# Band attention of a hybrid encoder layer: values as weights in two column halves for the prompt, column groups of 32 for the sample

## Chip, core and metric

The kernel runs on one core of one Trainium2 chip. The metric is the device time of one execution in microseconds (us). Three timed runs of the kernel before gave a median of 3266.02 us (3258.2 to 3266.6). One further execution was profiled; all rows below are from it.

## What is computed

One inference step of a one-layer encoder: 2048 prompt tokens (16 tiles of 128) and 8 x 16 sample tokens (one tile). Three residual sub-layers follow each other: a mixer with band attention (8 heads x 64) beside a convolution branch, cross-attention into 256 memory tokens, and an MLP. The change touches the band attention alone. Of the reference:

```python
def band_attn_prompt(q, k, v, table):      # per chunk of 64 queries, a band of 9 chunks of keys
    ...
    s = jnp.einsum('bnqhd,bnkhd->bnhqk', qc, kb).astype(jnp.float32) * (Dh ** -0.5)
    s = s + rel_bias(table, q_off, k_off).astype(jnp.float32)[None, None]
    s = jnp.where(key_valid[None, :, None, None, :], s, NEG_INF)
    p = jax.nn.softmax(s, axis=-1).astype(v.dtype)
    o = jnp.einsum('bnhqk,bnkhd->bnqhd', p, vb)
...
def band_attn_sample(q, k_all, v_all, table):   # 16 queries, 128 cached keys and 16 new ones
    s = jnp.einsum('bqhd,bkhd->bhqk', q, k_all).astype(jnp.float32) * (Dh ** -0.5)
    s = s + rel_bias(table, jnp.arange(T) + past, jnp.arange(L)).astype(jnp.float32)[None]
    p = jax.nn.softmax(s, axis=-1).astype(v_all.dtype)
    o = jnp.einsum('bhqk,bkhd->bqhd', p, v_all)
```

## The kernel before

The mixer takes the first 1010 us or so of the span, the tail of its output projection runs to about 1200 us beside the first cross-attention work, and the MLP fills the second half. Prompt tokens go in four quarters `q` of four tiles; the sample tile rides with quarter 0. For each quarter the input projection (`in_parts`, line L122) writes Q, K and V to scratch in DRAM (`Qd`, `Kd`, `Vd`), VectorE works off the 31 taps of the convolution (L451), and the attention of the quarter before is woven in between. `Plan` gives every small function a due time; sorted by it they are the program order, and a scheduler then sets the order on each engine, which holds at run time.

Most products run as three passes in fp32r (`mm3`: high x high, high x low, low x high). Those of the attention's second half are plain float32 matmuls, and each of them shows as two records of TensorE, with a weight load each.

Prompt attention, `attn(q)`: 32 steps, head `h` by head, tile `i` by tile. A step is `scores` (L564, into the only buffer `sc`; L568 on VectorE adds the bias and takes the minimum, L571 on ScalarE the exponential with its row sum), a step later `xpose` (L585, up to five 128x128 transposes of the probabilities; L587 copies them out), and another step later `values` (L597). There the transposed probabilities are the stationary operand, 128 wide, and 64 columns of V move past them: up to five matmuls a step, 560 in all. After a head's four steps VectorE divides by the row sums (L604). `attn_load` fetches a head's Q, K, V and bias ahead.

Sample attention, `sattn`: per stream `b` the cached keys are transposed (L653) and split, the new keys (L646) and the queries (L647) are loaded, GpSimd spreads the queries over a zeroed block `Q` (L642, L650), `sattn_scores` does 4 x 3 passes over 256 columns, and `sattn_values` (L689) does eight float32 matmuls with 128 wide V as the stationary operand and 32 moving columns.

The cross-attention of the sample tokens, which the change leaves alone, already uses column groups: `s_scores` (L927, tile `ssc`) and `s_values` (L965, tile `so`) give four matmuls with 32 columns of weights each the positions 0, 32, 64 and 96 of the array.

Of the kernel before, what the change touches and what calls it, by code (L numbers as in the profile page):

```python
# [73 lines left out]
class Kern:  # L74
# [93 lines left out]
    def mixer(self):  # L168
# [4 lines left out]
        with ExitStack() as st:  # L173
# [42 lines left out]
            def bias_tables():  # L216
# [14 lines left out]
                for h in range(H):  # L231
                    hk = mp.tile([P, 2, P], F32, tag="av", name="hk")
# [11 lines left out]
                hs = mp.tile([P, 2, P], F32, tag="av", name="hs")  # L244
# [284 lines left out]
            A, KQ, PEND, READY = {}, {}, [], []  # L529

            def attn_load(q, h):
                def fn():
# [8 lines left out]
                    vt = mp.tile([P, 8, HD], F32, tag="av", name="av")  # L541
# [3 lines left out]
                    ss = mp.tile([P, 4], F32, tag="ass", name="ass")  # L545
                    KQ[q, h] = (qt, kt, vt, bt, ss, k0)
                return fn

            def scores(q, h, i):
                def fn():  # L550
# [20 lines left out]
                    nc.scalar.activation(pr[:, :n], tt[:, :n], AF.Exp, bias=mn, scale=-1.0, accum_out=ss[:, i:i + 1])  # L571
# [5 lines left out]
            def xpose():  # L577
                q, h, i, pr, n, jo = PEND.pop(0)
                nj = n // P
                pt = mp.tile([P, 5, P], F32, tag="apt", name="apt")  # L580
# [7 lines left out]
                READY.append((q, h, i, pt, nj, jo))  # L588

            def values():  # L590
                q, h, i, pt, nj, jo = READY.pop(0)
                qt, kt, vt, bt, ss, k0 = KQ[q, h]
                if i == 0:
                    OC[q, h] = ps.tile([P, 4, HD], F32, tag="oc", name="oc")
                oc = OC[q, h]
                for j in range(nj):
                    nc.tensor.matmul(oc[:, i, :], pt[:, j, :], vt[:, jo + j, :], start=j == 0, stop=j == nj - 1)  # L597
                if i == 3:
                    if h % 2 == 0:
                        A[q] = mp.tile([P, 4, P], F32, tag="a", name="a")  # L600
                    r = mp.tile([P, 4], F32, tag="ar", name="ar")
                    nc.vector.reciprocal(r, ss)
                    c = (h % 2) * HD
                    nc.vector.tensor_tensor(A[q][:, :, c:c + HD], oc, r.unsqueeze(2).to_broadcast([P, 4, HD]), op=ALU.mult)  # L604
                    if h % 2:
                        t0 = QT[q][0]
                        nc.sync.dma_start(catd[t0 * P:(t0 + 4) * P, (h - 1) * HD:(h + 1) * HD].rearrange("(i p) c -> p i c", p=P), A[q])

            def attn(q):
                fns = [attn_load(q, 0)]  # L610
                for n in range(4 * H + 2):
                    h, i = n // 4, n % 4
                    if n < 4 * H:
                        fns.append(scores(q, h, i))
                    if 0 < n <= 4 * H:
                        fns.append(xpose)
                    if n > 1:
                        fns.append(values)
                    if i == 2 and h + 1 < H:
                        fns.append(attn_load(q, h + 1))  # L620
                return fns

# [3 lines left out]
            def sattn_prep():  # L626
                SA["vn"] = vn = mc.tile([P, DA], F32, tag="svn", name="svn")
                nc.sync.dma_start(vn, Vd[NTP * P:].rearrange("t h d -> t (h d)"))
                SA["aT"] = mp.tile([P, 4, P], F32, tag="saT", name="saT", bufs=1)

            def sattn_load(b):
                def fn():
                    tok = NTP * P
# [4 lines left out]
                    K = mp.tile([P, 4, 2, 256], F32R, tag="ak", name="sk")  # L638
                    Q = mp.tile([P, 4, 2, P], F32R, tag="sqb", name="sq")
                    qs = mp.tile([P, 4, 2, 16], F32, tag="a", name="qs")  # L640

                    nc.gpsimd.memset(fr(Q), 0.0)  # L642
# [11 lines left out]
                    self.split(K[:, :, 0, 0:P], K[:, :, 1, 0:P], pt.rearrange("p (j t) -> p j t", j=4))  # L654
                    SA[b] = (K, Q, cv)
                return fn

            def sattn_scores(b):
                def fn():
                    K, Q, cv = SA[b]  # L660
# [17 lines left out]
            def sattn_values(b):  # L678
                def fn():
# [4 lines left out]
                    PT = mp.tile([P, 2, P], F32, tag="apt", name="spt")  # L684
                    nc.scalar.activation(PT.rearrange("p s c -> p (s c)"), tp[:, :256], AF.Copy)
                    ov = ps.tile([P, 4, 32], F32, tag="oc", name="ov")
                    for p in range(4):
                        for s, vt in ((0, V), (1, SA["vn"])):
                            nc.tensor.matmul(ov[:, p], vt[:, p * P:(p + 1) * P], PT[:, s, p * 32:(p + 1) * 32], start=s == 0, stop=s == 1)  # L689
                    for j in range(2):  # L690
                        rs = slice(j * HD, (j + 1) * HD)
                        nc.vector.tensor_copy(SA["aT"][rs, :, b * 16:(b + 1) * 16], ov[rs, :, j * 16:(j + 1) * 16])
                    if b == 7:
                        tq = ps.tile([P, 512], F32, tag="tp", name="tpo", bufs=TPB)
                        for p in range(4):
                            nc.tensor.transpose(tq[:, p * P:(p + 1) * P], SA["aT"][:, p, :], self.ident)
                        so = mp.tile([P, DA], F32, tag="t512", name="so")
                        nc.scalar.activation(so, tq, AF.Copy)
                        nc.sync.dma_start(catd[NTP * P:, 0:DA], so)
# [714 lines left out]
```

## Time and profile before

| | |
|---|---|
| median of three runs | 3266.02 us |
| the profiled execution | 3256.27 us, span 3254.5 us |
| TensorE busy (matmul / weight load) | 96% / 82% of the span |
| VectorE, ScalarE, GpSimd busy | 56%, 38%, 19% |
| granted TensorE clock, mean | 0.985 of full speed |
| float32 value matmuls of the prompt (L597) | 1120 records, 319.5 to 1007.3 us |
| value matmuls of the sample (L689) | 128 records, 236.7 to 314.8 us |

Busy shares are averages over stages with different limits; what counts for the change is the stretch from about 210 us to 1010 us. A matmul's duration in a record holds its latency, so a rate is read from the starts of successive groups.

### The profile page before, as it was taken

To read this page: it belongs to the slowest core of one execution; us is meant where nothing else is said; L and a number is where in the kernel's file an instruction comes from. 1 tells how busy PE (TensorE), PEld (TensorE's weight loads), DVE (VectorE), ACT (ScalarE), POOL (GpSimd) and SP (SyncE) were. 2 spreads that over 40 slices of the span, in tenths; PEclk is the share of its full clock that TensorE was granted. 3 is DMA by queue.
4 is the path that set the end of the run, shared out by engine and by line. 5 is a ranking of instruction groups with operands and counts; after the bars stand their busy time and mean duration, and the time that the engine had idled before them with its cause. 6 is when DMAs were issued, how large, how long until landed. Compare 5 with 4: busy or idle time off the path is not lost. (4 is left out here: it accounts for less than half of the span.)

```text
span 3254.5 us, 44695 instructions
## 1 busy us (share of the span) xinstructions
PE 3129.9 (96%) x16664; PEld 2679.6 (82%) x16664; DVE 1827.2 (56%) x2812; ACT 1234.0 (38%) x2499; POOL 614.6 (19%) x704
## 2 busy tenths in 40 slices
PE   8889999999899999999999999999999999999998
PEld 7787788979898768788888999988888888888887
DVE  6798979788634435433335444455445544465444
ACT  3223454534554435422224232333334333343332
POOL 4346253342313320022221000002000200020000
PEclk9999999999899999999999999999999999999999
DMA  5465766747864565322224222234233432243222
GB/s 188 122 175 159 210 171 166 195 122 193 241 176 160 189 202 180 102 65 66 64 86 148 81 75 81 75 107 151 93 104 118 145 104 95 91 142 123 91 94 75
DMA packets 309352, 425.18 MB, mean 131 GB/s; under 512 B 62984, under 2 KB 177680, under 8 KB 309062
## 3 DMA queue, kind: packets, MB, share of 16 engines
q1 hardware_dynamic: 300574, 391.38, 40.5%
q0 software_dynamic: 8560, 30.94, 2.4%
q8 instruction: 131, 2.15, 0.3%
q14 instruction: 87, 0.71, 0.1%
HBM read 356.60 MB, written 69.52 MB: 131 GB/s over the span
## 5 line engine op out<-in xcount | busy, mean ns | idle before, releaser
L122 PE MATMUL pu<-xT,wu 128*128 128x512 f32 (+1 forms) x3840 | 756.3, 358 | 3.2 <-DVE xT L95 2.5
L122 PE MATMUL pd<-wd,h 128*128 128x512 f32 x3264 | 750.6, 390 | 1.4 <-DVE y L1336 1.1
L122 PEld LDWEIGHTS pu<-xT,wu 128*128 128x128 f32 x3840 | 659.9, 188 | 95.8 <-DVE xT L95 2.7
L122 PEld LDWEIGHTS pd<-wd,h 128*128 128x128 f32 x3264 | 611.3, 188 | 129.8 <-DVE y L1336 1.5
L122 PE MATMUL pm<-xT,w 128*128 128x512 f32 (+3 forms) x1992 | 423.2, 363 | 11.8 <-POOL w L95 6.2
L451 DVE SCALAR_TENSOR_TENSOR acc<-u,wdT,acc 128x512 f32<-128x512 f32 x480 | 429.7, 895 | 6.4
L103 POOL TENSOR_SCALAR nm<-nss 128x1 f32<-128x1 f32 x103 | 29.7, 288 | 2025.8 <-ACT nsq L132 1078.6
L122 PEld LDWEIGHTS pm<-xT,w 128*128 128x128 f32 x1992 | 337.6, 194 | 52.0 <-POOL w L95 6.5
L94 ACT ACTIVATE wd<-wst 128x512 fp32r<-128x512 f32 x256 | 159.8, 631 | 430.9 <-PE pd L122 364.5
L95 POOL TENSOR_TENSOR w<-wst,w 128x512 fp32r<-128x512 f32 x154 | 229.1, 1502 | 319.9 <-ACT w L94 296.2
L1336 DVE TENSOR_TENSOR y<-pd,y 128x512 f32<-128x512 f32 x238 | 163.5, 688 | 205.0 <-PE pd L122 204.9
L1318 DVE SCALAR_TENSOR_TENSOR hh<-pu,r 128x512 f32<-128x512 f32 (+1 forms) x160 | 96.8, 609 | 321.1 <-ACT r L1317 320.9
L1317 ACT ACTIVATE r<-pu 128x512 f32<-128x512 f32 (+1 forms) x160 | 83.8, 528 | 364.6 <-PE pu L122 356.5
L95 DVE TENSOR_TENSOR wu<-wst,wu 128x512 fp32r<-128x512 f32 x256 | 170.9, 690 | 86.7 <-ACT wu L94 85.7
L95 DVE TENSOR_TENSOR wd<-wst,wd 128x512 fp32r<-128x512 f32 x256 | 182.1, 735 | 35.7 <-ACT wd L94 35.1
L122 PE MATMUL pm<-wo,cT 128*128 128x512 f32 x816 | 200.4, 398 | 0.0
L94 ACT ACTIVATE wu<-wst 128x512 fp32r<-128x512 f32 x256 | 157.7, 630 | 100.6 <-DMA wst<-w_ffn_up 69.2
L122 PE MATMUL y<-mo,pT 128*128 128x512 f32 x768 | 187.1, 398 | 0.0
L122 PE MATMUL sc<-m,xT 128*128 128x512 f32 x768 | 182.0, 392 | 0.3 <-ACT xT L94 0.2
L122 PEld LDWEIGHTS pm<-wo,cT 128*128 128x128 f32 x816 | 151.3, 189 | 33.6 <-issue 2.9
L122 PEld LDWEIGHTS y<-mo,pT 128*128 128x128 f32 x768 | 142.9, 188 | 33.2
L122 PEld LDWEIGHTS sc<-m,xT 128*128 128x128 f32 x768 | 142.9, 188 | 30.8 <-DVE xT L95 0.5
(246 smaller groups left out, 3677.0 us busy)
## 6 DMA issues: line engine op xcount, KB each, us to landing
wst<-w_ffn_up SPq DMA_DIRECT2D x256, 256.0 KB, 3.2
wst<-w_ffn_down SPq DMA_DIRECT2D x256, 256.0 KB, 3.1
wst<-w_in SPq DMA_DIRECT2D x160, 256.0 KB, 3.9
ak<-Kd SPq DMA_DIRECT2D x48, 512.0 KB, 6.8
ab<-biasd SPq DMA_DIRECT2D x32, 320.0 KB, 4.2
cx<-catd SPq DMA_DIRECT2D x17, 512.0 KB, 7.4
x1d<-oy POOLq DMA_DIRECT2D x17, 512.0 KB, 5.9
nx<-x1d SPq DMA_DIRECT2D x17, 512.0 KB, 4.1
```

The costliest lines, as they stand in the source:

```text
L94: nc.scalar.activation(hi, src, AF.Copy)
L95: return (lo_eng or nc.vector).tensor_sub(lo, src, fr(hi))
L103: nc.gpsimd.tensor_scalar(m, ss, 1.0 / count, EPS, op0=ALU.mult, op1=ALU.add)
L122: self.nc.tensor.matmul(out, lhs(a), rhs(b), start=first and n == 0, stop=last and n == 2)
L451: i = nc.vector.scalar_tensor_tensor(o, s, wdT[:, c, w:w + 1], o, op0=ALU.mult, op1=ALU.add)
L1317: nc.scalar.activation(r, pm, AF.Relu)
L1318: nc.vector.scalar_tensor_tensor(hh, pm, 0.0, r, op0=ALU.max, op1=ALU.mult)
L1336: nc.vector.tensor_add(y, pm, y)
```

## The change

Prompt: `values` now takes two heads of a pair at once. V (64 columns) becomes the stationary operand and the transposed probabilities (128 columns) move; head 0 of the pair is put in the left column half of the array, head 1 in the right one. The result comes out transposed (head channels on partitions), so `heads_out` copies it to SBUF (ScalarE), transposes it with four more transposes per pair and quarter, and divides by the row sums. The 32 steps are walked in pairs of heads by `ORDER`, two heads are loaded ahead, and K of head `h + 2` is asked for behind the last `scores` of head `h`.

Sample: new keys and queries are loaded once for all streams and their high and low parts added; scores and values become plain float32 matmuls with 32 columns of weights in four column groups; the output is picked by a mask and written per stream.

```diff
-                    vt = mp.tile([P, 8, HD], F32, tag="av", name="av")
+                    vt = mp.tile([P, 8, HD], F32, tag="av", name="av", bufs=3)
...
-                for j in range(nj):
-                    nc.tensor.matmul(oc[:, i, :], pt[:, j, :], vt[:, jo + j, :], start=j == 0, stop=j == nj - 1)
...
-                    nc.vector.tensor_tensor(A[q][:, :, c:c + HD], oc, r.unsqueeze(2).to_broadcast([P, 4, HD]), op=ALU.mult)
...
+            def values(q, g, i):
+                def fn():
+                    if i == 0:
+                        OC[q, g] = ps.tile([P, 4, P], F32, tag="oc", name="oc")
+                    oc = OC[q, g]
+                    hs = [READY.pop((q, 2 * g + x, i)) + (KQ[q, 2 * g + x][2],) for x in range(2)]
+                    nj = hs[0][1]
+                    for j in range(nj):
+                        for x, (pt, _, jo, vt) in enumerate(hs):
+                            nc.tensor.matmul(oc[x * HD:(x + 1) * HD, i, :], vt[:, jo + j, :], pt[:, j, :], start=j == 0, stop=j == nj - 1,
+                                             tile_position=(0, x * HD))
+                    if i == 3:
+                        ot = mp.tile([P, 4, P], F32, tag="t512", name="ot")
+                        nc.scalar.activation(ot, oc, AF.Copy)
...
+            def heads_out(q, g):
+                def fn():
+                    ot, ss = OC.pop((q, g)), SUM.pop((q, g))
+                    tp = ps.tile([P, 512], F32, tag="tp", name="tpv", bufs=TPB)
+                    for i in range(4):
+                        nc.tensor.transpose(tp[:, i * P:(i + 1) * P], ot[:, i, :], self.ident)
+                    r = mp.tile([P, 4, 2], F32, tag="ar", name="ar")
+                    nc.vector.reciprocal(r, ss)
+                    A = mp.tile([P, 4, P], F32, tag="a", name="a")
+                    nc.vector.tensor_tensor(A.rearrange("p i (x d) -> p (i x) d", x=2), tp.rearrange("p (n d) -> p n d", d=HD),
+                                            r.rearrange("p i x -> p (i x)").unsqueeze(2).to_broadcast([P, 8, HD]), op=ALU.mult)
...
+            ORDER = ((0, 0), (0, 1), (1, 0), (0, 2), (1, 1), (0, 3), (1, 2), (1, 3))
+                steps = [(2 * g + x, i) for g in range(H // 2) for x, i in ORDER]
+                fns = [attn_load(q, 0), attn_load(q, 1)]
...
+                        if i == 3 and h + 2 < H:
+                            fns.append(attn_load(q, h + 2))
...
+                s = mp.tile([P, 2, 4, 2, P], F32, tag="ak", name="skq")
+                            nc.sync.dma_start(s[j * HD:(j + 1) * HD, x, :, a, :], src.rearrange("(p j) a d t -> j a d p t", j=2)[j, a, :, :, tok:tok + P])
+                nc.vector.tensor_tensor(q, s[:, 1, :, 0, :], s[:, 1, :, 1, :], op=ALU.add)
...
-                        for a in range(2):
-                            nc.sync.dma_start(fr(K)[rs, :, a, P:256], Kd.rearrange("(p j) a d t -> j a d p t", j=2)[j, a, :, :, tok:tok + P])
-                            nc.sync.dma_start(qs[rs, :, a, :], Qd.rearrange("(p j) a d t -> j a d p t", j=2)[j, a, :, :, tok + b * 16:tok + b * 16 + 16])
-                        for p in range(4):
-                            c = (2 * p + j) * 16
-                            nc.gpsimd.tensor_copy(Q[rs, p, :, c:c + 16], qs[rs, p])
+                        nc.gpsimd.tensor_copy(Z[rs, :, j * 16:(j + 1) * 16], SA["q"][rs, :, b * 16:(b + 1) * 16])
...
-                    self.split(K[:, :, 0, 0:P], K[:, :, 1, 0:P], pt.rearrange("p (j t) -> p j t", j=4))
+                    nc.scalar.activation(K[:, :, 0:P], pt.rearrange("p (j t) -> p j t", j=4), AF.Copy)
...
-                        self.mm3(sp, lambda x: Q[:, p, x, :], lambda y: K[:, p, y, :], p == 0, p == 3)
+                        nc.tensor.matmul(sp[p * 32:(p + 1) * 32], Z[:, p, :], K[:, p, :], start=True, stop=True, tile_position=(0, p * 32))
...
-                            nc.tensor.matmul(ov[:, p], vt[:, p * P:(p + 1) * P], PT[:, s, p * 32:(p + 1) * 32], start=s == 0, stop=s == 1)
+                            nc.tensor.matmul(ov[p * 32:(p + 1) * 32], PT[:, s, p * 32:(p + 1) * 32], vt[:, p * P:(p + 1) * P], start=s == 0, stop=s == 1,
+                                             tile_position=(0, p * 32))
...
+                    nc.vector.tensor_scalar(so, ov[:, 0:HD], SA["m"][:, 0:1], None, op0=ALU.mult)
+                    nc.vector.scalar_tensor_tensor(so, ov[:, HD:P], SA["m"][:, 1:2], so, op0=ALU.mult, op1=ALU.add)
```

On TensorE, in the attention of the last quarter beside the output projection (`pm<-wo...`, one piece of w_out), this stood before: each step's five value matmuls `oc`, 64 columns wide, next to the transposes `tpa` and the scores `sc`.

```order
L564 MATMUL sc<-ak,aq 128x320 x4
L585 MATMUL tpa<-ident,apr 128x128 x5
L597 MATMUL oc<-av,apt 128x64 x5
L564 MATMUL sc<-ak,aq 128x320 x4
L122 MATMUL pm<-wo_9042,cT 128x512 x2
L585 MATMUL tpa<-ident,apr 128x128 x5
L597 MATMUL oc<-av,apt 128x64 x5
```

In the same place of the change the value matmuls stand ten at a time (or split by other work), 64 wide and with 128 columns moving.

```order
L565 MATMUL sc<-ak,aq 128x320 x4
L586 MATMUL tpa<-ident,apr 128x128 x5
L601 MATMUL oc<-apt,av 64x128 x10
L565 MATMUL sc<-ak,aq 128x320 x4
L586 MATMUL tpa<-ident,apr 128x128 x5
L601 MATMUL oc<-apt,av 64x128
L122 MATMUL pm<-wo_8873,cT 128x512
L565 MATMUL sc<-ak,aq 128x320 x4
L601 MATMUL oc<-apt,av 64x128 x4
L586 MATMUL tpa<-ident,apr 128x128 x5
L601 MATMUL oc<-apt,av 64x128 x5
```

The first row of ten is a whole step of two heads; the second step of two is broken in three by other work. Over all quarters the 560 matmuls of L601 stand in 99 unbroken runs, 48 of which have an odd number of matmuls.

On TensorE, in the sample attention (`sps` are the scores, `ov` the values, `pm<-xT,w` the input projection of quarter 1), this stood before for one stream:

```order
L122 MATMUL sps<-sk,sq 128x256 x12
L122 MATMUL pm<-xT,w 128x512 x15
L653 MATMUL pt<-ident,sck 128x128 x4
L683 MATMUL tps<-ident,spr 128x128 x2
L122 MATMUL pm<-xT,w 128x512 x4
L689 MATMUL ov<-spt,scv 128x32
L689 MATMUL ov<-spt,svn 128x32
```

The pair of `ov` rows stands there four times in a row. In the change:

```order
L701 MATMUL sps<-sk,sz 32x256 x4
L122 MATMUL pm<-xT,w 128x512 x17
L691 MATMUL pt<-ident,sck 128x128 x4
L721 MATMUL tps<-ident,spr 128x128 x2
L122 MATMUL pm<-xT,w 128x512 x2
L701 MATMUL sps<-sk,sz 32x256
L727 MATMUL ov<-scv,spt 32x128 x4
L727 MATMUL ov<-svn,spt 32x128 x4
L701 MATMUL sps<-sk,sz 32x256 x3
```

Twelve matmuls of 256 columns become four in four column groups, and eight of 32 columns become eight of 128 columns in four groups. The sample's new matmuls stand in 12 unbroken runs; for two streams the scores are broken as one and three.

## Rows read from the trace of the kernel before

**Rows 1.** The page: busy time, share of the span and instructions of the engines.

```profile
PE 3129.9 (96%) x16664; PEld 2679.6 (82%) x16664; DVE 1827.2 (56%) x2812; ACT 1234.0 (38%) x2499; POOL 614.6 (19%) x704
```

**Rows 2.** Stretches: us, then busy us of PE, PEld, DVE, ACT, POOL; clock, DMA.

```profile
236.00:280.00 44.00, 40.18 (x246) 34.83 (x245) 31.93 (x64) 18.44 (x39) 33.22 (x53) 0.96 0.54 147
280.00:320.00 40.00, 36.06 (x205) 29.70 (x205) 37.83 (x61) 13.38 (x30) 27.31 (x31) 0.96 0.60 155
...
500.00:550.00 50.00, 47.00 (x281) 41.17 (x280) 48.19 (x70) 22.84 (x53) 17.61 (x16) 1.00 0.62 156
...
700.00:750.00 50.00, 50.00 (x310) 43.94 (x309) 43.85 (x69) 25.74 (x58) 15.00 (x10) 1.00 0.65 175
```

**Rows 3.** Tile `sc`, then tile `sq`: idle time before their instructions, and its releaser.

```profile
  DVE amn L568: 51.6, 37
...
  POOL sq L650: 5.7, 6
```

**Rows 4.** Tile `oc`: the value matmuls, ns min/median/max, first and last start.

```profile
L597 PE MATMUL oc<-av,apt x1120: 217/275/475, 319.5 to 1007.3; 128*128 128x64 f32 x187
```

**Rows 5.** Timeline of PE: start us, us, group. Ten value records, then the projection.

```profile
599.83 1.23 PE L597 MATMUL oc<-av,apt 128*128 128x64 f32 x10
600.87 3.07 PE L122 MATMUL pm<-w,xT 128*128 128x256 f32 x24
```

**Rows 6.** Timeline of PE: column groups of 32 in the sample's cross-attention.

```profile
1168.16 0.73 PE L122 MATMUL pm<-wo,cT 128*128 128x512 f32 x2
1168.82 1.07 PE L965 MATMUL so<-sv,spT 128*32 128x256 f32 x16
...
1170.41 0.62 PE L927 MATMUL ssc<-skT,z 128*32 128x256 f32 x2
1170.96 0.44 PE L973 MATMUL pt<-ident,sob 128*128 128x128 f32 x2
...
1185.19 1.07 PE L965 MATMUL so<-sv,spT 128*32 128x256 f32 x16
1186.20 1.09 PE L916 MATMUL pt<-ident,sk 128*128 128x128 f32 x8
1187.22 0.94 PE L927 MATMUL ssc<-skT,z 128*32 128x256 f32 x6
```

**Rows 7.** The chain that ended last: start us, us, undisturbed transposes and fp32r matmuls.

```profile
2147.13 0.87 PE pt L144 x8
...
2162.55 21.80 PE pu L122 x96
```

**Rows 8.** Timeline of PE: one stream's sample scores, and one stream's sample values.

```profile
221.51 1.58 PE L122 MATMUL sps<-sk,sq 128*128 128x256 f32 x12
222.93 3.15 PE L122 MATMUL pm<-xT,w 128*128 128x512 f32 x13
...
236.68 0.41 PE L689 MATMUL ov<-spt,scv 128*128 128x32 f32 x2
...
238.48 0.71 PE L122 MATMUL pm<-xT,w 128*128 128x512 f32 x2
```

**Rows 9.** Groups by line and form: busy us, mean ns; idle before, releaser.

```profile
L604 DVE TENSOR_TENSOR a<-oc,ar 128x256 f32<-128x256 f32 x32 | 13.4, 418 | 16.9 <-PE oc L597 16.9
...
L650 POOL CAST sq<-qs 64x32 fp32r<-64x32 f32 x64 | 21.1, 371 | 0.5
...
L487 ACT ACTIVATE lnd<-pt 128x512 f32<-128x512 f32 x17 | 9.9, 591 | 8.9 <-PE pt L485 6.1 <-DVE lnd L505 2.5 <-DMA catd<-lnd 0.3
```

**Rows 10.** SP's waits, us in total, times, longest; issues of K with KB and us to landing.

```profile
SPq L542 <- PE oc L597: 67.6, 9, 15.0
...
ak<-Kd SPq DMA_DIRECT2D x48, 512.0 KB, 6.8
```

**Rows 11.** Stretches of tile `oc` alone: us, then busy us (records) of PE, PEld, DVE.

```profile
410.00:600.00 190.00, 35.69 (x272) 34.81 (x273) 2.92 (x7) 0.96 0.66 175
600.00:850.00 250.00, 48.01 (x390) 47.39 (x389) 4.16 (x10) 0.98 0.64 173
...
885.00:1010.00 125.00, 32.91 (x260) 32.16 (x260) 2.96 (x7) 0.99 0.58 163
```

More of the change, by code (lines that the diff above doesn't have):

```diff
@@ L570, in fn @@
                     pr = mp.tile([P, 640], F32, tag="apr", name="apr")
-                    nc.scalar.activation(pr[:, :n], tt[:, :n], AF.Exp, bias=mn, scale=-1.0, accum_out=ss[:, i:i + 1])
+                    nc.scalar.activation(pr[:, :n], tt[:, :n], AF.Exp, bias=mn, scale=-1.0, accum_out=ss[:, i, h % 2:h % 2 + 1])
                     PEND.append((q, h, i, pr, n, j0 - k0))
@@ L609, in attn @@
-            def attn(q):
[L610 to L615, printed above, removed]
-                        fns.append(xpose)
[L617 to L620, printed above, removed]
+                READY[q, h, i] = pt, nj, jo
@@ new lines, in mixer @@
+            ORDER = ((0, 0), (0, 1), (1, 0), (0, 2), (1, 1), (0, 3), (1, 2), (1, 3))
+            def attn(q):
+                steps = [(2 * g + x, i) for g in range(H // 2) for x, i in ORDER]
+                fns = [attn_load(q, 0), attn_load(q, 1)]
+                for n in range(len(steps) + 3):
+                    if n < len(steps):
+                        fns.append(scores(q, *steps[n]))
+                    if 0 < n <= len(steps):
+                        fns.append(xpose)
+                    if 1 < n < len(steps) + 2:
+                        h, i = steps[n - 2]
+                        if h % 2:
+                            fns.append(values(q, h // 2, i))
+                    if n > 2:
+                        h, i = steps[n - 3]
+                        if h % 2 and i == 3:
+                            fns.append(heads_out(q, h // 2))
+                    if n < len(steps):
+                        h, i = steps[n]
+                        if i == 3 and h + 2 < H:
+                            fns.append(attn_load(q, h + 2))
@@ L626, in sattn_prep @@
             def sattn_prep():
+                tok = NTP * P
                 SA["vn"] = vn = mc.tile([P, DA], F32, tag="svn", name="svn")
-                nc.sync.dma_start(vn, Vd[NTP * P:].rearrange("t h d -> t (h d)"))
-                SA["aT"] = mp.tile([P, 4, P], F32, tag="saT", name="saT", bufs=1)
+                nc.sync.dma_start(vn, Vd[tok:].rearrange("t h d -> t (h d)"))
+                SA["m"] = m = mc.tile([P, 2], F32, tag="smask", name="smask")
+                nc.gpsimd.memset(m, 0.0)
+                for p in range(4):
+                    nc.gpsimd.memset(m[p * 32:p * 32 + 16, 0:1], 1.0)
+                nc.gpsimd.tensor_scalar(m[:, 1:2], m[:, 0:1], -1.0, 1.0, op0=ALU.mult, op1=ALU.add)
+                s = mp.tile([P, 2, 4, 2, P], F32, tag="ak", name="skq")
+                for j in range(2):
+                    for a in range(2):
+                        for x, src in enumerate((Kd, Qd)):
+                            nc.sync.dma_start(s[j * HD:(j + 1) * HD, x, :, a, :], src.rearrange("(p j) a d t -> j a d p t", j=2)[j, a, :, :, tok:tok + P])
+                SA["q"] = q = mp.tile([P, 4, P], F32, tag="saT", name="saq", bufs=1)
+                K = mp.tile([P, 2, 4, 256], F32, tag="ak", name="sk")
+                SA["k"] = [K[:, n] for n in range(2)]
+                nc.vector.tensor_tensor(q, s[:, 1, :, 0, :], s[:, 1, :, 1, :], op=ALU.add)
+                for k in SA["k"]:
+                    nc.vector.tensor_tensor(k[:, :, P:256], s[:, 0, :, 0, :], s[:, 0, :, 1, :], op=ALU.add)
+                z = mp.tile([P, 2, 4, 32], F32, tag="sqb", name="sz", bufs=1)
+                nc.gpsimd.memset(z, 0.0)
+                SA["z"] = [z[:, n] for n in range(2)]
             def sattn_load(b):
                 def fn():
-                    tok = NTP * P
                     ck = mp.tile([P, DA], F32, tag="att", name="sck")
@@ L683, in fn @@
                         nc.tensor.transpose(tp[:, s * P:(s + 1) * P], pr[:, s * P:(s + 1) * P], self.ident)
[L684 removed]
+                    PT = mp.tile([P, 2, P], F32, tag="apt", name="spt", bufs=4)
                     nc.scalar.activation(PT.rearrange("p s c -> p (s c)"), tp[:, :256], AF.Copy)
[L686 to L699 removed]
+                    ov = ps.tile([P, P], F32, tag="oc", name="ov")
+                    for s, vt in ((0, V), (1, SA["vn"])):
+                        for p in range(4):
+                            nc.tensor.matmul(ov[p * 32:(p + 1) * 32], PT[:, s, p * 32:(p + 1) * 32], vt[:, p * P:(p + 1) * P], start=s == 0, stop=s == 1,
+                                             tile_position=(0, p * 32))
+                    so = mp.tile([P, HD], F32, tag="a", name="so")
+                    nc.vector.tensor_scalar(so, ov[:, 0:HD], SA["m"][:, 0:1], None, op0=ALU.mult)
+                    nc.vector.scalar_tensor_tensor(so, ov[:, HD:P], SA["m"][:, 1:2], so, op0=ALU.mult, op1=ALU.add)
+                    r0 = NTP * P + b * 16
+                    nc.sync.dma_start(catd[r0:r0 + 16, 0:DA].rearrange("t (h d) -> h t d", h=H), so)
                 return fn
```

42 lines of the change are left out of this document (15 added, 27 removed).

## The prediction

> **What bounds the kernel now.** I read the page first, then stretches of the mixer, then what TensorE waited for, then the value matmuls one by one. The page shows TensorE busy 96% of the span [rows 1]; nothing else is near. By stretches the picture is less simple. From 700 to 750 us TensorE is busy all 50.00 us, but from 280 to 320 us VectorE is busy 37.83 of 40 us against 36.06 on TensorE, and from 500 to 550 us 48.19 of 50 against 47.00 [rows 2]. So the two are coupled: TensorE sat idle 51.6 us in all before instructions on the single score buffer `sc` until VectorE's minimum was done [rows 3]. Work taken off TensorE is worth its full price where VectorE has slack, and becomes a longer wait for `sc` where it has none. The MLP and the cross-attention behind 1010 us are not touched.
>
> **Prompt values on TensorE.** Before: ten records (five matmuls of two records each) start at 599.83 and the next group at 600.87, 1.04 us, or 0.104 us a record [rows 5]; 1120 records [rows 4] are 116.5 us. After: the same 560 matmuls, 64 wide, 128 columns moving, two halves. No matmul in column halves is in the trace; the nearest rows are the quarters of 32 columns [rows 6]. There one matmul alone (two records, 256 columns each, in one group) takes 0.55 us to the next group's start (1170.41 to 1170.96), and sixteen records (eight matmuls, so four records in each of four groups) take 1.01 us (1185.19 to 1186.20). Four streams against two: (1.01 - 0.55) / 2 = 0.23 us a stream of 256 columns, however many groups run it, and 0.09 us once a run. I take half, 0.115 us, for 128 columns. Neighbours pay too: eight transposes between two such runs take 1.02 us (1186.20 to 1187.22) where undisturbed ones take 0.87 [rows 6, 7], 0.15 us more; two fp32r matmuls of 512 columns between two runs take 0.66 us (1168.16 to 1168.82) where 2 x 21.80 / 96 = 0.45 is the undisturbed price, 0.21 us more. So a run costs 0.24 to 0.30 us besides its streams; I take 0.27, since both kinds of neighbour occur. The order gives 99 runs, and in 48 one matmul has no partner: 560 + 48 = 608 streams x 0.115 = 69.9, plus 99 x 0.27 = 26.7, is 96.6 us. **Relief 19.9 us.** If the halves did not overlap it would be 1120 x 0.115 + 26.7 = 155.5 us, 39.0 us more than before; this is the bound on the other side.
>
> **`heads_out`.** 4 transposes for each of 16 pairs at 0.87 / 8 = 0.109 us [rows 7]: **7.0 us more** on TensorE. The ScalarE copy, 16 x 0.591 us by the nearest copy out of PSUM of that shape [rows 9], is 9.5 us on an engine with half its time free (22.84 of 50 us [rows 2]); the transposes wait for it, but in 15 of the 16 places other matmuls or transposes stand between the last value matmul and them. Without that cover it would be about 0.9 us a place (copy plus handing over), 14 us in all. VectorE's division: 32 x 0.418 before, 16 with twice the elements after, so about the same.
>
> **Sample on TensorE.** Scores took 222.93 - 221.51 = 1.42 us a stream and values 238.48 - 236.68 = 1.80 us [rows 8], 25.8 us for eight. After: scores two streams of 256 columns, values four of 128: 4 x 0.23 = 0.92 us, 7.4 for eight; two broken scores cost 2 x 0.46 more; 12 runs x 0.27 = 3.2. Sum 11.5 us, **relief 14.3 us**. The four last transposes (0.4 us) fall away too.
>
> **Sample elsewhere.** GpSimd loses 64 casts (21.1 us [rows 9]) and eight clearings, and gets 16 copies of twice the elements (some 6 to 12 us by the same row). TensorE's 5.7 us of waiting for those casts [rows 3] goes. VectorE loses eight splits and gains three adds and a few small operations, a gain of a few us at most. SP issues eight loads of new keys and queries in place of 64.
>
> **Loads.** Values now free V two heads at a time, and V has three buffers; SP stood 67.6 us behind that wait before [rows 10]. K of head h + 2 now waits for the last scores of head h, and on SP the weights of the projection are queued behind it. It has three steps to arrive; 128 steps in the 688 us of [rows 4] are 5.4 us each, so 16 us, against 6.8 us to landing [rows 10] and a few issues. I cost it at nothing; the cover is those 16 us.
>
> **The sum.** Relief on TensorE: 19.9 - 7.0 + 14.3 + 0.4 + 5.7 = 33.3 us. What of it reaches the end goes by stretch. Behind 600 us, where TensorE is full, lie about 0.65 of the value records (390 and 260 of 1120 in the two stretches shown, 80 more between them [rows 11]): 0.65 x 12.9 = 8.4 us, all of it. From 410 to 600 us 272 records, 3.1 us, of which I take half, since VectorE is nearly full there [rows 2]. The other 21.8 us (the sample and the first quarter's start) fall between 210 and 410 us, where VectorE is busy 73 to 95% [rows 2]; I take just over half, 12 us, since VectorE and GpSimd get lighter as well. Together 22 us. The profiled execution took 3256.3 us; after, 3234. The median of the runs lies 9.7 us above the profiled one, so on its scale 3266 - 22 = **3244 us**. The likeliest case's own range is all of the relief to a third of it: 3233 to 3255.
>
> **Rivals.**
> - *VectorE takes it back.* Only the 8.4 us behind 600 us reach the end: 3258, no measurable change (0.3%, 10 us, is about what a measurement of this kernel tells from none). For it: the 51.6 us on `sc` and the full VectorE at 280 and 500 us [rows 2, 3]. Against: the sample's part also takes work from VectorE.
> - *The weight load is not hidden in a half.* If a 64-column load could not run under its own column half's stream, each stream would be longer by half the 0.104 us that the 128-column load sets the pace with now [rows 5]: 608 x 0.167 + 26.7 = 128 us, 12 us more than before; the sample's 52 streams would cost 0.026 more each. Relief -11.7 - 7.0 + 12.9 + 6.1 = 0.3: 3266. Against it: a 256-column stream took 0.23 us, as long as an undisturbed 512-column fp32r matmul (21.80 / 96 = 0.227), which leaves no room for a load of even 32 columns (0.026) [rows 6, 7]. The Trainium skill, "TensorE: Matmul & The Clock Gate", Part 3, states that a weight load overlaps matmuls in flight only when the row groups differ, and column halves share all rows. By that rule this rival would be the case; the rows of the quarters don't bear it out, so I give it little.
> - *The halves take turns* (the other side): 39.0 us more on the values, and 7.0 for the transposes, less the sample's 20.4: 25.6 us longer, 3291 if all of it reaches the end. It decides from the point where a run of ten matmuls takes 2.0 us rather than 1.4. Against it: four quarters ran at once in [rows 6].
> - *Late loads.* If the load of K behind the scores came 1 us late for each of the 24 heads that it is asked for this way, 24 us of waiting would outweigh the gain: 3268. For it: K is 512 KB and lands in 6.8 us only at the median [rows 10].
>
> **Chances.** Forecast 0.62; VectorE 0.18; load not hidden 0.05; turns 0.05; late loads 0.10. The first gives faster, except for its weak end; the second and third about the same; the last two are slower or the same. Faster 0.65, same 0.20, slower 0.15. To leave out no more than 2 in 10 the range reaches from above the full relief (3233, with 7 us for a lighter GpSimd and VectorE) to the late loads: 3226 to 3268.
>
> **What would show it.** In the new profile a run of ten value matmuls (20 records) should take 1.3 to 1.5 us from its start to the next group's; 2.0 or more shows a hidden load lost or turns. The sample scores should take about 0.6 us a stream. `tpv` should wait for ScalarE for a few us in all. The idle time before `sc` on VectorE's account should grow by no more than some 10 us; if it grows by 25, the first rival is right. Waits of the scores on loads of K or Q should stay absent. Wrong altogether would be a stretch from 600 to 850 us that is not shorter.

## The result, and the profile after

The changed kernel takes 3285.64 us (median of 4 runs, 3280.49 to 3287.35) against 3262.11 us (4 runs): a ratio of 1.0065, 95% interval 1.0048 to 1.0081. It is **slower by 0.65%, 23.5 us by the medians**, where 3244 us, 22 us faster, was forecast. The profiled execution took 3285.85 us, span 3283.3 us, mean granted clock 0.977.

The page's row of busy time answers to [rows 1]:

```profile
PE 3113.4 (95%) x16692; PEld 2613.2 (80%) x16692; DVE 1813.1 (55%) x2775; ACT 1242.0 (38%) x2514; POOL 589.7 (18%) x655
```

TensorE has 16.5 us less work in a span that is 28.8 us longer, so the loss is idle time (169.9 us against 124.6) and clock, not work. By stretches, as in [rows 2] (us, busy us of PE, PEld, DVE, ACT and POOL, clock, DMA):

```profile
236.00:280.00 44.00, 33.88 (x240) 24.71 (x244) 26.38 (x58) 16.34 (x37) 24.38 (x32) 0.84 0.59 171
280.00:320.00 40.00, 30.63 (x191) 22.66 (x180) 32.98 (x51) 17.05 (x35) 31.57 (x30) 0.92 0.49 149
500.00:550.00 50.00, 46.77 (x280) 37.82 (x281) 48.09 (x72) 21.76 (x50) 14.38 (x13) 0.97 0.61 147
700.00:750.00 50.00, 42.26 (x242) 34.35 (x241) 43.14 (x64) 20.38 (x48) 11.80 (x8) 0.86 0.48 125
```

The stretch from 700 to 750 us, full before, now has 7.7 us of idle TensorE at a clock of 0.86 (the projection's last copy into `u` starts 8 us later than before, at 708.0 us; VectorE is as busy as it was). The idle time before the two score tiles, `sc` and then `sps`, by what ended it, answers to [rows 3]:

```profile
  DVE amn L569: 85.2, 60
```

```profile
  POOL sz L688: 18.7, 2
```

By this view the wait for VectorE's minimum grew by 33.6 us over the 51.6 of [rows 3]. But the view of a tile adds the idle time before the weight loads to that before the matmuls, so it counts a gap of TensorE twice where both waited. The waits of the matmuls alone, before and after (us in total, times, longest), are smaller:

```profile
PE sc L564 <- DVE amn L568: 24.2, 13, 7.2
```

```profile
PE sc L565 <- DVE amn L569: 36.8, 26, 4.6
```

TensorE waited 12.6 us longer for the minimum, and the 51.6 us that the prediction took for its idle time were 24.2. In the same way the 18.7 us are one gap of 9.2 us before the first sample scores, which start at 243.4 us where they stood at 221.51 [rows 8]. A run of value records on TensorE's timeline, beside [rows 5]:

```profile
575.83 1.31 PE L601 MATMUL oc<-apt,av 128*64 128x128 f32 x20
577.07 0.86 PE L565 MATMUL sc<-ak,aq 128*128 128x320 f32 x4
```

Twenty records take 1.24 us to the next group; two runs of ten were 2.08. The part that the forecast worked hardest on came out a little cheaper than priced, and the kernel is slower all the same.

### The profile page after: what moved, and what is told of

Read it like the earlier page. It is cut to its first block, busy times and chain, and to the rows that moved or that the text cites. A ratio compares the mean times of both kernels' runs of the same rounds, so it can differ in the third digit from the quotient of the medians.

```text
span 3283.3 us, 44540 instructions
## 1 busy us (share of the span) xinstructions
PE 3113.4 (95%) x16692; PEld 2613.2 (80%) x16692; DVE 1813.1 (55%) x2775; ACT 1242.0 (38%) x2514; POOL 589.7 (18%) x655
## 5 line engine op out<-in xcount | busy, mean ns | idle before, releaser
L451 DVE SCALAR_TENSOR_TENSOR acc<-u,wdT,acc 128x512 f32<-128x512 f32 x480 | 428.2, 892 | 7.0
```

The costliest lines, as they stand in the source:

```text
L451: i = nc.vector.scalar_tensor_tensor(o, s, wdT[:, c, w:w + 1], o, op0=ALU.mult, op1=ALU.add)
```

## The experiments

Three theories went in: the loss comes from new waits of the prompt part in the last quarter; any disturbance of the hand-set due times costs as much; the walk in pairs with its late loads is the loss. Differences are to the median of the kernel before that was measured beside the run, since that median moves between 3261.09 and 3263.36 us. The medians are of 2 to 10 runs (of 2 for the halves in blocks), and by the ratios a difference comes out up to 3 us otherwise than by the medians.

| run | median, us | before, us | ratio, 95% interval |
|---|---|---|---|
| sample part alone | 3251.68 | 3261.29 | 0.9961 (0.9947 to 0.9976) |
| and larger pools | 3263.72 | 3261.29 | 1.0000 (0.9990 to 1.0009) |
| and walk in pairs | 3270.95 | 3261.29 | 1.0030 (1.0019 to 1.0041) |
| (and column halves: the change) | 3285.64 | 3262.11 | 1.0065 (1.0048 to 1.0081) |
| due times shifted, no other change | 3275.81 | 3261.29 | 1.0035 (1.0020 to 1.0049) |
| change, early tables in two buffers | 3267.30 | 3263.36 | 1.0015 (1.0005 to 1.0026) |
| change, `ot` on VectorE | 3283.12 | 3263.36 | 1.0065 (1.0050 to 1.0080) |
| change, w_out cast on GpSimd | 3291.23 | 3263.36 | 1.0091 (1.0075 to 1.0106) |
| change, halves in blocks | 3286.65 | 3263.36 | 1.0076 (1.0056 to 1.0096) |
| early tables, one w_out transfer | 3259.19 | 3261.09 | 0.9992 (0.9981 to 1.0004) |
| sample part, one w_out transfer | 3248.70 | 3261.09 | 0.9961 (0.9946 to 0.9976) |
| early tables, last tiles 6 earlier | 3261.28 | 3261.09 | 0.9994 (0.9984 to 1.0004) |
| early tables, w_out 8 later | 3277.84 | 3261.09 | 1.0047 (1.0030 to 1.0064) |
| sample part and pools, early tables in two | 3252.59 | 3261.31 | 0.9970 (0.9955 to 0.9985) |
| walk in pairs, early tables in two | 3260.41 | 3261.31 | 1.0000 (0.9988 to 1.0011) |
| last four tiles in the old form | 3259.67 | 3261.31 | 0.9994 (0.9984 to 1.0004) |

### The change taken up step by step

The kernel before, with the new sample functions and nothing else:

```
-            def sattn_prep(): ... def sattn_values(b): ...   (as before)
+            def sattn_prep(): ... def sattn_values(b): ...   (as changed)
```

> The kernel before with the sample part of the change alone (column groups of 32, new keys loaded once), the prompt part as before. Theory 1 (the loss comes from the prompt part's new waits in the last quarter; the sample part loses 9 us ahead of its first scores and wins it back): between 5 us faster and 8 us slower than before. Theory 2 (any disturbance of the tuned due times costs this much): 10 to 25 us slower. Theory 3 (the walk in pairs of heads, with its later loads, is the loss): like theory 1 here.

Measured: 3251.68 us, 9.6 us faster, more than theory 1 allowed. It beats both kernels, and its first sample scores start at 221.7 us. Next, the larger pools:

```
-mp.tile([P, 2, P], F32, tag="av", name="hk")   # hs and av likewise; apt and spt: two buffers
+mp.tile([P, 2, P], F32, tag="av", name="hk", bufs=3)   # apt and spt: bufs=4
```

> As the sample part alone, and also a third buffer for V and four for the transposed probabilities, nothing else of the prompt part. Theories 1 and 3: within 5 us of the sample part alone, perhaps a little faster since SP waits less for V. Theory 2: again 10 to 25 us slower than before, with no order between the two.

Measured: 3263.72, so the pools give the whole gain back with no change of work, which fits none of the three theories. The first sample scores start at 243.7 us. Next, the order in head pairs with the loads of the change, values in their old form:

```
-fns = [attn_load(q, 0)]
+steps = [(2 * g + x, i) for g in range(H // 2) for x, i in ORDER]
+fns = [attn_load(q, 0), attn_load(q, 1)]
```

> As the one before, and also the walk in pairs of heads with two heads loaded ahead and K asked for behind the last scores; the value matmuls keep the old form (probabilities as weights, 64 columns moving, no column halves, no transposes of the result). Theory 1: at most 10 us slower than before. Theory 3: 15 to 25 us slower, as much as the whole change. Theory 2: 10 to 25 us slower.

Measured: 3270.95, 7 us more, with one wait of 7.8 us for K between 840 and 900 us. That is 9.7 us above the kernel before, within theory 1 and short of theory 3. And the kernel before with only the attention's due times moved:

```
-as1=27.1, as2=41.1, as3=8.8, ae0=183.0, ae1=2.4, ae2=12.1, ae3=102.6
+as1=29.1, as2=43.1, as3=10.8, ae0=185, ae1=4.4, ae2=14.1, ae3=104.6
```

> The kernel before with no change in its work: only the due times of the attention of all quarters are moved by 2 units (their starts and ends). Theory 2: 10 to 25 us slower. Theories 1 and 3: within 8 us of before.

Measured: 3275.81, 14.5 us slower without a single instruction changed, only their order. That any disturbance costs so much falls, since the sample part alone is faster; but a shift of the due times is worth two thirds of the whole forecast. No run set them anew for the change, so the prices of its parts below hold for these due times only.

### The early tables

```
-mp.tile([P, 2, P], F32, tag="av", name="hk", bufs=3)   # hs likewise
+mp.tile([P, 2, P], F32, tag="a", name="hk")            # two buffers, as before the change
```

> The changed kernel, with the tables hk and hs of the first 200 us put into the two buffers of the division's output instead of the three of the values: the early transposes then follow each other as they did before the change. If the third buffer of the early tables is what made the first sample scores wait (244 us against 222, one gap of 9.2 us under GpSimd's sz, and 12 us in the run that only added buffers to the sample part), that gap goes, the first sample scores start before 230 us, and the time falls by 8 to 14 us, to 3272 to 3278. If the loss lies wholly behind 600 us (waits of the prompt part), the first sample scores come earlier but the time stays within 4 us of the changed kernel.

Measured: 3267.30. Of 23.5 us above the kernel before, 3.9 are left: **19.6 us hang on one more buffer for tables that are done with before the sample's scores begin.** More than the 8 to 14 expected, and none of the three theories had it. Between the two profiled executions lie 15.0 us (spans of 3283.3 and 3268.3): 9.8 of them are idle time of TensorE, about the one gap of 9.2 us, and 5.2 the same work at a lower mean clock (busy 3113.4 and 3108.2 us, clock 0.977 and 0.982). GpSimd's timeline in the changed kernel (start, us, group, idle time and releaser):

```profile
229.38 1.76 POOL L95 TENSOR_TENSOR w<-wst,w 128x512 fp32r<-128x512 f32 x1
242.47 1.84 POOL L688 COPY sz<-saq 64x64 f32<-64x64 f32 x4 [11.33 <-DVE saq L671]
```

VectorE in the changed kernel, and then in the run above:

```profile
240.46 0.74 DVE L451 SCALAR_TENSOR_TENSOR acc<-u,wdT,acc 128x512 f32<-128x512 f32 x1
...
241.72 0.68 DVE L671 TENSOR_TENSOR saq<-skq 128x512 f32<-128x512 f32 x1
```

```profile
217.73 0.74 DVE L451 SCALAR_TENSOR_TENSOR acc<-u,wdT,acc 128x512 f32<-128x512 f32 x1
...
219.86 0.68 DVE L671 TENSOR_TENSOR saq<-skq 128x512 f32<-128x512 f32 x1
```

In the changed kernel the add that makes `saq` stands behind 231 instructions of the convolution (L451) on VectorE, with two buffers for the tables behind 206, and comes 21.9 us later; GpSimd, in order, waits for it with `w`'s splits queued behind, and the sample scores wait for GpSimd. Why the third buffer moves it back was not traced further (the loads of `skq` are issued later too, the last at 221.7 instead of 213.1 us). The edit changes the tag of the tables as well as the number of their buffers; but the sample part alone, with two buffers under the old tag, starts its scores at 221.7 us too, so it is the number that counts. The same edit on the run with the sample part and the pools:

> The sample part of the change and the larger pools of values and copies (3264 us with the early tables in them, 3252 without the pools), with the early tables hk and hs in the two buffers of the division's output. If the third buffer harms only by letting the early transposes run ahead, the time goes back to 3249 to 3255; if a larger pool disturbs the prompt part itself, it stays above 3259.

Measured: 3252.59, within a microsecond of the sample part alone. The larger pools harm through the early tables only. Here the edit gives back 11.2 us, and 10.6 on the walk in pairs below, where it gave 19.6 on the whole change. By the intervals that can be scatter; or the tables and the column halves cost together what neither costs alone.

### The last quarter

The changed kernel, one edit each; first the copy out of PSUM:

```
-nc.scalar.activation(ot, oc, AF.Copy)
+nc.vector.tensor_copy(ot, oc)
```

> The changed kernel, with the copy ot out of PSUM on VectorE instead of ScalarE; nothing else. If the loss of the last step is ScalarE, which holds ot behind the casts of w_out that wait for their transfers (tpv waited 9.6 us for ot, oc 23.9 us for apt), the wait under ot goes and the time falls by 3 to 8 us. If VectorE paces the prompt part (sc waited 85.2 us for amn), 16 copies of some 0.7 us more on it cost 3 to 10 us. If neither, within 3 us.

Measured: the same ratio as the change, 1.0065. From 840 to 1060 us `tpv` waits 1.7 us for the copy instead of 4.7, but `tpa` waits 7.6 us for the exponential (`apr`) instead of 0.4: another wait took the place of the first.

```
-self.split(w[:, 0], w[:, 1], s)     # ScalarE, then VectorE
+nc.gpsimd.tensor_copy(w[:, 0], s)   # three pieces asked for ahead
+nc.vector.tensor_sub(w[:, 1], s, fr(w[:, 0]))
```

> The changed kernel, with the first halves of w_out's eight pieces cast on GpSimd instead of ScalarE, three pieces asked for at the start and each next one behind a cast. ScalarE then has nothing between 850 and 890 us that waits for w_out. If its casts hold apt and ot there (three gaps of TensorE of 4.3 to 4.7 us), those gaps go, the granted clock of 860 to 900 rises from 0.65 to 0.75 towards 0.9, and the time falls by 8 to 16 us. If VectorE, which still takes the second halves in order, or the transfers of K and V beside w_out are the limit there, sc's wait for amn takes the gaps over and the time stays within 4 us.

Measured: 3291.23, which is 27.9 us above the kernel before where the change is 23.5. From 840 to 1060 us the wait of `oc` for `apt` falls from 8.9 to 0.2 us and that of `tpv` from 4.7 to 1.2, but `sc` waits 19.1 us for the minimum instead of 6.3. That is the second branch: the waits moved and grew, so ScalarE's queue alone is not the cause. What TensorE waited for from 850 to 1060 us in the changed kernel (us in total, times, longest):

```profile
PE oc L601 <- ACT apt L588: 8.9, 3, 4.4
PE sc L565 <- DVE amn L569: 6.3, 5, 3.5
PE tpv L614 <- ACT ot L605: 4.7, 1, 4.7
...
PE oc L601 <- DMA av<-Vd: 2.2, 1, 2.2
PE sc L565 <- DMA ak<-Kd: 1.6, 1, 1.6
```

Next the transfers themselves, on the run with the early tables mended, and on the sample part alone:

```
+if k == 0:
     s = op.tile(...); nc.gpsimd.dma_start(s, I["w_out"][0, k * P:(k + 1) * P, :])
```

> The run with the early tables in two buffers (3267 us), leaving out seven of w_out's eight transfers: the first piece is cast eight times, so the output projection takes a wrong weight. That kernel is 7 us ahead of the kernel before at score 96 (842 us) and 15 us behind at the middle of the output projection (1063 us). If w_out's 4 MB, which share the DMA engines with the loads of K, Q, V and the tables there and hold ScalarE and VectorE, are what costs those 22 us, the time falls by 14 to 24 us, to 3243 to 3253. If the walk in head pairs costs them by itself (order of the scores, late loads), it falls by less than 8 us.

> The run with the sample part of the change alone (3252 us), leaving out the same seven transfers of w_out. By the theory that the old walk, which asks for one head at a time, leaves room for w_out, it gains little here: 0 to 8 us. If it gains as much as the run above (14 us or more), w_out's transfers cost every order the same and are not what sets the two apart.

Measured: 3259.19 (8.1 us less, 5.8 by the differences to before) and 3248.70 (3.0 less, 2.8 by the differences). The first is at the edge of "less than 8 us" and far from 14: w_out costs the pairs some 3 to 5 us more than the old walk, near what the intervals can tell, and not 22. From 840 to 960 us, with the early tables mended, then without seven of the transfers (columns as above):

```profile
840.00:960.00 120.00, 96.78 (x584) 77.07 (x581) 48.73 (x82) 61.89 (x138) 22.88 (x32) 0.83 0.72 197
```

```profile
840.00:960.00 120.00, 101.75 (x664) 81.35 (x665) 55.69 (x94) 70.51 (x161) 25.29 (x30) 0.90 0.65 177
```

TensorE gets through more records (664 against 584), at a clock of 0.90 against 0.83. Two moves of the due times on the same kernel:

```
-as3=8.8
+as3=2.8
```

> The run with the early tables in two buffers, with the attention of the last four tiles due 6 units earlier, so that its first two heads are asked for ahead of w_out. If the collision of two heads' loads with w_out behind 850 us is the loss, the time falls by 6 to 15 us, to 3252 to 3261; if the prompt part is simply paced by VectorE or ScalarE there, it stays within 5 us or rises, since the scores then crowd into the projection ahead.

```
-wa=14.8, wb=24.7
+wa=22.8, wb=32.7
```

> The run with the early tables in two buffers, with w_out's transfers and casts due 8 units later, behind the first scores of the last four tiles. If the collision is the loss, the first scores of that part run without waits and the time falls by 4 to 12 us, unless the output projection then waits for w_out (its first tile came at 904 us), which would give back as much: then within 5 us or slower.

Measured: 3261.28 (6 us less, 3.7 by the differences) and 3277.84 (some 13 more by the differences). The first lies at the edge between its two branches and decides nothing. In the second the last minimum of the prompt part starts 14.7 us earlier (at 1002.4 instead of 1017.1 us), so w_out's transfers and casts do hold that part back. But the output projection starts at 903.5 instead of 893.6 us, and behind 1000 us TensorE waits for `nx`, which the output projection feeds, 11.6 us at one time:

```profile
PE pt L144 <- DVE nx L134: 14.7, 2, 11.6
```

### Pairs and halves by themselves

With the early tables out of the way:

> The walk in head pairs with the values in their old form (3271 us), with the early tables in the two buffers of the division's output. Beside the run with the column halves and the same early tables (3267 us) it has every part of the change but the halves. If the halves' relief of some 13 us on TensorE, after the copies back, reaches the end, this run is 8 to 15 us slower than 3267; if the relief is absorbed by the waits, within 5 us; if the halves cost (as 3271 to 3286 in the old early order says), it is 8 to 18 us faster, at 3249 to 3259.

Measured: 3260.41. The walk in pairs costs 7.8 us against 3252.59, and the column halves, on top of it, another 4.8 (differences to before of -0.9 and +3.9 us). That is between the second and the third branch: the halves do not gain, and whether they lose is near what the intervals can tell. TensorE's waits in this run contain one late load of K:

```profile
PE sc L564 <- DMA ak<-Kd: 7.3, 1, 7.3
```

It is the first head of the last four tiles: its K is asked for at 840.2 us, among w_out's transfers (asked for from 837.0 to 869.4 us), and lands at 854.0.

Two stretches of this run, and of the same with column halves (columns as above):

```profile
236.00:840.00 604.00, 553.06 (x3561) 485.41 (x3562) 505.35 (x789) 278.92 (x636) 237.38 (x194) 0.96 0.62 166
840.00:960.00 120.00, 101.69 (x632) 91.89 (x631) 54.32 (x96) 66.10 (x150) 24.84 (x34) 0.86 0.75 206
```

```profile
236.00:840.00 604.00, 542.13 (x3616) 447.39 (x3618) 510.40 (x773) 284.33 (x652) 234.88 (x193) 0.97 0.62 168
```

And the matmuls' wait for VectorE's minimum in the two:

```profile
PE sc L564 <- DVE amn L568: 25.8, 19, 7.1
```

```profile
PE sc L565 <- DVE amn L569: 36.7, 25, 3.9
```

With the halves TensorE is busy 10.9 us less in the same 604 us and gets 3 us further (the last copy into `u` starts at 691.6 us against 694.8): most of the relief has turned into waiting, and `sc` waits 10.9 us more over the whole kernel. The starts of VectorE's minimums, 128 in all, show where the halves gain and lose. The 64th, the 96th and the last start at 632.6, 843.4 and 1008.6 us without the halves, and at 625.2, 841.3 and 1017.1 with them: 7.4 us ahead, 2.1 ahead, 8.5 behind. So the relief arrives in the first half and is lost behind it, most of it in the last four tiles. There TensorE waits for ScalarE's copies (840 to 1060 us, with the halves):

```profile
PE oc L601 <- ACT apt L588: 7.8, 3, 4.4
PE sc L565 <- DVE amn L569: 6.3, 5, 3.5
PE tpv L614 <- ACT ot L605: 4.4, 1, 4.4
```

Without the halves the first two are 1.6 and 3.9 us, and there is no third. The converse test makes TensorE's value work dearer without touching any other engine:

```
-for j in range(nj):
-    for x, (pt, _, jo, vt) in enumerate(hs):
+for x, (pt, _, jo, vt) in enumerate(hs):
+    for j in range(nj):
```

> The changed kernel, with the 20 records of a run in two blocks: first the 10 of one head in its column half, then the 10 of the other head, instead of in turn; the same instructions and buffers. If the two halves work at the same time only when their records stand in turn, a run of 20 goes from 1.24 us to 2.0 to 2.6 us, TensorE gets 60 to 110 us more work by the price of 99 runs, and the kernel 30 to 100 us slower than the changed one. If a record in a half costs half of one over all columns by itself (no work at the same time), the run stays at 1.2 to 1.3 us and the time within 4 us.

The timeline of a run, and the matmuls' wait for the minimum:

```profile
584.43 2.02 PE L601 MATMUL oc<-apt,av 128*64 128x128 f32 x20
586.38 0.97 PE L122 MATMUL pm<-xT,w 128*128 128x512 f32 x3
```

```profile
PE sc L565 <- DVE amn L569: 25.3, 20, 3.7
```

Twenty records now take 1.95 us instead of 1.24. If all 1120 records stood in whole runs that would be 1120 / 20 x 0.71 = 40 us more on TensorE, an estimate; many runs are shorter, and the page has 27.8 us more (3141.2 us busy against 3113.4). The run length is just short of the first branch of the expectation, the time is that of the second: 3286.65 us (two runs), a ratio of 1.0076 where the change has 1.0065. TensorE's idle time is 23.7 us less, 11.5 of it before `sc`. **Some 28 us more on the value matmuls hardly move the end**: they fill idle time that was there, half of it the wait for VectorE's minimum.

Last, twelve tiles in pairs and halves and the last four in the old form:

```
-pl.add(t + Z["as3"], t + Z["ae3"], attn(3))
+pl.add(t + Z["as3"], t + Z["ae3"], attn1(3))   # one head at a time, values as before
```

> The run with the early tables in two buffers (3267 us), where the last four tiles alone go back to one head at a time and the old value form; the other twelve tiles keep the pairs and the column halves. By the theory that the whole loss behind score 96 comes from pairs and halves beside w_out, the time falls by 12 to 20 us, to 3247 to 3255, at or a little below the sample part alone (3252). If the pairs and halves lose in the first three quarters too, it stays above 3258.

Measured: 3259.67, about 5.5 us less by the differences to before, and 8 above the sample part alone. That is the second branch, just above 3258: the last four tiles in the new form account for less than half of the pairs' and halves' 12.6 us. The rest shows at the joint to those tiles. From the 96th minimum to the 97th, the first of the last four tiles, 18.0 us pass in this run, where 8.3 pass in the one with the sample part, the pools and the tables in two buffers.

## Why the prediction was wrong

**The step that failed is the sum.** It took TensorE's relief, 33.3 us, and let 22 of it reach the end, by how full TensorE was in each stretch; the new buffers and the new order of loads stood in it at nothing. Two things were wrong with that.

- *Terms put at nothing.* "Loads" follows the third buffer of the values only in what it frees for V. The early tables share that buffer's tag. Through them it moves the sample's add back on VectorE around 220 us and costs 19.6 us, the larger part of the loss (10.6 to 11.2 in the kernels without the halves). The changed kernel's instruction order was read for TensorE only, not for VectorE. The walk in pairs, in the same paragraph and also at nothing, costs 7.8.
- *A full stretch was read as a TensorE-bound one.* Behind 600 us all of the prompt's 8.4 us was to arrive. Instead the halves lose there: from the 64th minimum to the last, 391.9 us pass with them and 376.0 without. That TensorE was full because the plan filled each wait of the attention with projection work is the likely reason, but no run shows it. Two engines' waits came out instead: VectorE's minimum (36.8 us of the matmuls' time against 24.2 before) and, in the last four tiles, ScalarE's copies.

The text said that growth of 25 us before `sc` would make the first rival right. The row that it names grew by 33.6, of which TensorE's matmuls waited 12.6. The rival is right that VectorE takes relief of the prompt part back, and wrong in which relief: it let the 8.4 us behind 600 us arrive and not the sample's, and it was the sample's that arrived (9.6 us). Its time, 3258, is 9 us below the 3267 of the run with the early tables mended; the walk in pairs was not in it. The mark "wrong altogether" is met too: from the 64th minimum to the 96th, about 640 to 850 us, 215.6 us pass in the changed kernel and 211.6 before.

**Two readings.** The 51.6 us of [rows 3] are 24.2 of the matmuls and 27.5 of the weight loads, mostly the same gaps. The 5.7 us of waiting for casts in the sum are 2.1 of the matmuls and 3.6 of the weight loads:

```profile
PE sps L122 <- POOL sq L650: 2.1, 1, 2.1
```

So that term was too large by 3.6 us, which is little beside the miss.

**Runs of value matmuls**: right in mechanism and a little dear, 1.24 us where 1.3 to 1.5 was expected. Runs of two, ten and twenty records (two, six and ten streams one after the other) take 0.36, 0.80 and 1.24 us, which is 0.11 us a stream, as priced, and 0.14 us a run besides; what a run's neighbours pay was not read. Net of the copies back, the halves take 9.4 us off TensorE's busy time (3117.6 without, 3108.2 with them, early tables mended), where 12.9 was forecast. The rivals of a load that is not hidden and of halves that take turns fall by the same row; the rule of the Trainium skill quoted for the first ("TensorE: Matmul & The Clock Gate", Part 3) would, taken alone, have made runs dearer, and 1.24 us for twenty records does not agree with it. That the run's length decides from 2.0 us was not put to the test: at 1.95, just short of it, the time is the same.

**The sample part**: right. Its relief of 14.3 + 0.4 + 5.7 us gives 9.6 us alone, close to the half that was taken, and its scores take 0.55 to 0.57 us in five of the eight streams where 0.6 was expected.

**`heads_out`**: on TensorE a little under its price, 0.36 us for four transposes in most places where 0.44 was taken. Its cover was missing in one of the sixteen places (`tpv` waited 4.7 us), as the text allowed; moving the copy to VectorE did not change the time.

**Late loads**: a rival with 0.10, and near the truth by luck. It is not 1 us for each of the 24 heads that are asked for behind the scores, but 7.3 us for one that is not among them, the first head of the last four tiles, asked for beside w_out. In the changed kernel that wait is 1.6 us, and the place shows waits for `apt` and `ot`; that these come from the same collision is not shown. The walk as a whole costs 7.8 us; which share of it is that one wait was not separated.

By the differences to before, the account is: sample part -9.6, pools without the early tables +0.9, walk in pairs +7.8, column halves +4.8, early tables +19.6; together +23.5 us. These are steps along one path and add up by construction; by the ratios they are -12.7, +2.9, +9.8, +4.9 and +16.3. Taken in the other order, the tables cost 10.6 and the halves 13.9. That the halves lose at all is a matter of less than a shift of the due times moves (14.5).

## What to carry to other kernels

Relief on the busiest engine counts only after the wait beside it has been checked: make that engine's work dearer for one run, and if the time stays, its work is not what sets the end. Take the wait from the matmuls alone, since a tile's view adds the weight loads' idle time to theirs. Follow an added buffer to every tile that shares its tag, and read the new instruction order at all of them, on the engines off the path as well. In a kernel whose order is tuned by hand, keep the parts that gain alone (here the sample part, 3251.68 us) and compare the rest against them.

## What the runs showed of the hardware

- float32 matmuls in two column halves overlap when their records alternate between the halves (1.24 us for twenty) and less when each half's ten stand together (1.95 us); one tile position a matmul is not enough, the order of issue decides.
- Waits cost more than their length in these runs. Of the 15.0 us between the profiled executions with and without the early tables mended, 5.2 are the same work at a lower mean clock (0.977 against 0.982). From 840 to 960 us TensorE was busy 96.78 us at a granted clock of 0.83 with w_out's transfers, and 101.75 us at 0.90 without seven of them; the clock there is a mean of its two levels, 1.2 and 2.4 GHz. The busy share of a stretch does not set the clock alone: with the last four tiles in the old form TensorE is busy 107.44 us of the same stretch, and the clock is 0.83 as well:

```profile
840.00:960.00 120.00, 107.44 (x636) 95.74 (x634) 51.76 (x93) 64.02 (x143) 25.12 (x34) 0.83 0.76 205
```
